# Projection tiles as 512-column matmuls on both weight parts, their halves added by VectorE, and the exponential's bias made by ScalarE

## The chip, the cores and the metric

The kernel runs on one core of a Trainium2 chip. The metric is the device time of one execution in microseconds; the number given for a kernel is the median of its runs. The profile is one execution taken apart by the hardware profiler. Its engines are PE (TensorE, matmuls; PEld is its weight load), DVE (VectorE), ACT (ScalarE), POOL (GpSimd) and SP (SyncE, which issues the DMAs).

## What is computed

One encoder layer on two groups of 1024 rows ("prompt", then "sample") that share their weights. Cut to what matters here:

```python
h = rms_norm(x, norm_g) * (1.0 + scale) + shift
proj = jnp.einsum('bsd,de->bse', h, w_in)              # 1024 -> 5376 columns
qa, ka, va, za, qb, kb, vb, zb, ga, gb = jnp.split(proj, ...)
qa, ka, qb, kb = rms_norm per head of 64, gain, rotary positions
oa = gqa_attention(qa, ka, va) * silu(za)              # 8 q heads, 2 kv heads
ob = rms_norm(diff_attention(qb, kb, vb, lam)) * silu(zb)   # 4 heads, two maps each
merged = sigmoid(ga) * (oa @ w_proj_a) + sigmoid(gb) * (ob @ w_proj_b)
y = x + gate * (merged @ w_out)
```

The softmax of a row of scores s is exp(rs * s - rs * max(s)), with rs the query row's inverse root mean square, which the kernel keeps apart and applies here.

## The kernel before

**Three products for one.** Every large product is made of 32-bit values that are split in a high part (a copy rounded to the matmul's type) and a low part (the rest): x * w becomes xh*wh + xh*wl + xl*wh, three matmuls added up in one PSUM bank. `split_w` (L190) splits a weight tile: ScalarE makes the high part (L195) and GpSimd or VectorE the low part (L197). A weight tile is laid out as [128, 8 chunks, 2 parts, 256 columns], so both parts of a chunk are 512 columns side by side.

**Projections by rows** (`proj_tt`, L565) are the place of the change. A tile is 128 rows of h by 256 columns of `w_in`. h (transposed, in `u` tiles) is the stationary side, so the result has rows on partitions. Over eight chunks of 128 channels run the three matmuls of L574, 128x256 each: 24 to a tile. The bank comes from `fbank`, a pool of three that projections, gates, transposes and others share. There are 72 such tiles to a group: 8 for k and v of branch A (`kva_gen`), 16 for its q (`qa_gen`), 32 for q and k of branch B (`qkb_gen`), 16 for its v (`vb_gen`).

**What reads a tile.** For v of branch B, one ScalarE copy (L749) takes it out of the bank. For q and k, `rms` (L586) does: ScalarE copies (L591) and squares (L592), VectorE sums the squares (L595) and adds epsilon (L596), GpSimd raises to the power -1/2 (L597), and `rope` rotates. In the heads of a group (`alone`) the rotation is VectorE's, elsewhere GpSimd's. `kva_gen` takes v out of the same bank by another ScalarE copy (L689). The rows then go back to TensorE to be transposed (`pairs_T`, L637), two tiles later (LAG).

**Softmax** (`softmax_unit`, L790). Four matmuls (L798, L799) fill one of two score banks `s` with 1024 scores for 128 rows. VectorE finds the negative maximum (L800) and scales it by rs (L801); ScalarE makes the exponential with it as bias (L802), which frees the bank. VectorE transposes the result in blocks of 32 (L843), DMAs carry it, and TensorE multiplies with the values (L866 and L883). There are 256 such units.

**The order of the work.** `weave` merges streams (attention steps, projections, gates by `z_gen` at L764) in shares that tables at the head of the file set, and the recorded program is then put in order engine by engine by a scheduler that follows priorities and its own idea of when operands are ready. Each engine runs its own list strictly in order. An edit to one function can therefore move instructions everywhere.

The functions that the change touches, and those that call them:

## Time and profile before

| | |
|---|---|
| median of 3 runs | 1882.31 us (1879.48 to 1884.93) |
| span of the profiled execution | 1880.0 us |
| TensorE busy | 98% of the span, 10398 matmuls |
| VectorE busy | 65% |
| ScalarE busy | 41% |
| GpSimd busy | 32% |
| mean granted clock of TensorE | 0.995 |

The span is the time from the first to the last instruction of the profiled execution; the runs were timed apart from it. A group row of the profile has the line, the engine, the operation, the tiles (out<-in), the shape and the count, then the busy time in us, the mean of one in ns, and the idle time of the engine ahead of these instructions with what ended most of it. Matmuls overlap each other in the array, so their busy time is longer than the time from one start to the next.

### The profile page before, as it was taken

The page shows a single profiled execution, that of the slowest core. Times are in us where ns is not written, and L with a number is a line of the kernel's source. Part 1 is how long each engine was busy: PE and PEld are TensorE (multiplying, and loading weights), DVE is VectorE, ACT ScalarE, POOL GpSimd, SP SyncE. Part 2 cuts the span into 40 slices and gives each one's busy share as a digit, 9 for nine tenths or more (in the row PEclk, how much of TensorE's full clock was granted, in tenths as well). Part 3 has the DMA queues.
Part 4 walks back from the last instruction along what each step waited for, and adds up shares of the span by engine and source line. Part 5 has one row for each costly group of instructions (what it writes and reads, how often), then busy time and mean ns, then how long its engine had stood idle before and what let it go on. Part 6 is the DMA issues. An engine that isn't in the chain of part 4 may idle for free.

```text
span 1880.0 us, 29891 instructions
## 1 busy us (share of the span) xinstructions
PE 1836.5 (98%) x10398; PEld 1550.6 (82%) x10398; DVE 1222.3 (65%) x2016; ACT 780.1 (41%) x1544; POOL 607.1 (32%) x888
## 2 busy tenths in 40 slices
PE   6999999999999999999999999999999999999999
PEld 3798877888899977888889888888888898888887
DVE  5777766454777777347466687666357766663795
ACT  4544434344554444313223445344345545442241
POOL 1243311433454451221233333014354635222100
PEclk8999999999999999999999999999999999999999
DMA  9135776555444567754631567666524343675442
GB/s 324 57 94 160 208 198 178 146 168 163 111 127 113 162 188 219 244 152 140 206 131 52 156 177 204 189 186 188 158 68 141 106 129 103 176 247 173 128 127 92
DMA packets 283895, 295.46 MB, mean 157 GB/s; under 512 B 41952, under 2 KB 236640, under 8 KB 283744
## 3 DMA queue, kind: packets, MB, share of 16 engines
q1 hardware_dynamic: 283744, 293.54, 53.1%
q8 instruction: 83, 1.36, 0.3%
q14 instruction: 68, 0.56, 0.1%
HBM read 133.98 MB, written 42.01 MB: 94 GB/s over the span
## 4 chain that ended last, share of the span: by engine, by line
PE 68%; DMA 4%; issue 3%; DVE 3%; SPq 3%; POOL 2%; ACT 1%; ACTq 0%; DVEq 0%; POOLq 0%
PE f L764 15%; PE f L574 15%; PE f L1038 7%; PE a L883 5%; PE s L798 4%; PE s L799 4%; PE a L866 4%; PE s L1038 3%; PE f L1073 3%; PE s L1073 2%; PE f L1145 2%; SPq L852 1%; DMA q<-p 1%; DMA st<-in_w_in_dram 1%; PE s L1145 1%
## 5 line engine op out<-in xcount | busy, mean ns | idle before, releaser
L764 PE MATMUL f<-u,w 128*128 128x512 f32 x2232 | 565.1, 395 | 0.8 <-POOL w L197 0.4
L574 PE MATMUL f<-w,u 128*128 128x256 f32 x3456 | 478.6, 287 | 0.9 <-POOL w L197 0.4
L764 PEld LDWEIGHTS f<-u,w 128*128 128x128 f32 x2232 | 409.8, 188 | 82.6 <-POOL w L197 1.1
L574 PEld LDWEIGHTS f<-w,u 128*128 128x128 f32 x3456 | 452.3, 193 | 22.3 <-issue 3.5
L800 DVE TENSOR_REDUCE m<-s 128x1 f32<-128x1024 f32 x256 | 309.6, 1218 | 98.8 <-PE s L799 97.4
L197 POOL TENSOR_TENSOR w<-st,w 128x512 fp32r<-128x512 f32 x160 | 213.2, 1350 | 357.9 <-ACT w L195 342.1
L843 DVE STREAM_TRANSPOSE p<-p 128x1024 f32<-128x1024 f32 x192 | 237.7, 1243 | 87.9 <-ACT p L802 73.5
L802 ACT ACTIVATE p<-s,m,u 128x1024 f32<-128x1024 f32 x128 | 153.9, 1204 | 160.0 <-issue 57.8
L802 ACT ACTIVATE p<-s,m,rsB 128x1024 f32<-128x1024 f32 x128 | 154.0, 1204 | 118.7 <-DVE m L801 97.1
L799 PE MATMUL s<-u,sw 128*128 128x512 f32 x512 | 201.1, 397 | 0.0
L195 ACT ACTIVATE w<-st 128x512 fp32r<-128x512 f32 x184 | 108.2, 626 | 112.4 <-DMA st<-in_w_in_dram 97.5
L1038 PE MATMUL f<-u,w 128*128 128x512 f32 x552 | 131.0, 392 | 0.0
L883 PE MATMUL a<-q,u 128*128 128x256 f32 x512 | 126.5, 380 | 4.0 <-DMA q<-p 3.7
L597 POOL TENSOR_TENSOR rsB<-ss,nhalf 128x4 f32<-128x4 f32 x64 | 68.1, 1064 | 184.7 <-DVE ss L596 160.6
L866 PE MATMUL a<-q,u 128*64 128x256 f32 x1024 | 117.7, 382 | 3.6 <-DMA q<-p 2.9
L1038 PEld LDWEIGHTS f<-u,w 128*128 128x128 f32 x552 | 103.0, 188 | 21.1
L798 PE MATMUL s<-u 128*128 128x512 f32 x256 | 107.9, 425 | 2.7 <-ACT p L802 2.7
L799 PEld LDWEIGHTS s<-u,sw 128*128 128x128 f32 x512 | 96.5, 189 | 16.4
L640 DVE TENSOR_TENSOR u<-f,u 64x256 fp32r<-64x256 f32 (+1 forms) x198 | 81.3, 411 | 42.9 <-ACT u L639 37.5
L883 PEld LDWEIGHTS a<-q,u 128*128 128x128 f32 x512 | 93.5, 190 | 18.8 <-issue 3.4
L772 ACT ACTIVATE ev<-f 128x512 f32<-128x512 f32 x93 | 55.3, 595 | 128.5 <-PE f L764 72.5
L866 PEld LDWEIGHTS a<-q,u 128*64 128x64 f32 x1024 | 73.8, 137 | 40.3 <-issue 7.2
(221 smaller groups left out, 2174.6 us busy)
## 6 DMA issues: line engine op xcount, KB each, us to landing
q<-p SPq DMA_DIRECT2D x768, 128.0 KB, 2.6
st<-in_w_in_dram SPq DMA_DIRECT2D x132, 256.0 KB, 3.3
zd<-ev SPq DMA_DIRECT2D x96, 256.0 KB, 2.7
sw<-u SPq DMA_DIRECT2D x256, 64.0 KB, 2.0
u<-in_w_ada_dram SPq DMA_DIRECT2D x8, 1024.0 KB, 11.7
oo<-zd SPq DMA_DIRECT2D x64, 128.0 KB, 2.4
od<-oo SPq DMA_DIRECT2D x64, 128.0 KB, 2.4
st<-in_w_in_dram SPq DMA_DIRECT2D x64, 128.0 KB, 2.7
```

The source lines that it names most:

```text
L195: hi = nc.scalar.activation(wh, st, AF.Copy)
L197: lo = e.tensor_tensor(out=wl, in0=st, in1=wh.bitcast(F32), op=ALU.subtract)
L574: ins = nc.tensor.matmul(ps, lt[c][:, sl], w[:, c, wi, :], start=(k == 0), stop=(k == 23))
L764: ins = nc.tensor.matmul(ps, w[:, c, wi, e * P : (e + 1) * P], rt[c], start=(k == 0), stop=(k == 23),)
L798: nc.tensor.matmul(s[:, sl], q, k[:, sl], start=True, stop=False)
L799: nc.tensor.matmul(s[:, sl], sw, k[:, sl], start=False, stop=True)
L800: nc.vector.tensor_reduce(out=m, in_=s, axis=AX.X, op=ALU.max, negate=True)
L802: nc.scalar.activation(pt.rearrange("p (j c a) -> p j c a", j=4, c=8), s.rearrange("p (c a j) -> p j c a", c=8, j=4), AF.Exp, bias=m, scal ...
L843: nc.vector.transpose(pt, pt)
L866: lambda k=k, m=m: nc.tensor.matmul(acc[(LO, HI)[m]], u["v"][:, k], pT[m][:, k], start=(k == 0), stop=(k == 7))
L883: nc.tensor.matmul(acc, u["v"][:, k], pT[:, k], start=(k == 0), stop=(k == 7))
L1038: nc.tensor.matmul(ps, w[:, c, wi, d * P : (d + 1) * P], o[:, oi, :], start=(k == 0), stop=(k == 11))
```

## The change

In `proj_tt` the high part of the rows now meets both weight parts in one matmul of 512 columns, and the low part meets the high weights in one of 256 columns that adds to the second half of the bank: 16 matmuls to a tile in place of 24. The bank then holds xh*wh in its first half and xh*wl + xl*wh in the second. A new function `summed` copies the first half out by ScalarE and lets VectorE add the second half to the copy, in place; `rms` and `vb_gen` use it in place of the single copy. In `kva_gen` v is copied from the summed row in SBUF instead of from the bank, inside `rms`. Epsilon is added by GpSimd instead of VectorE. In `softmax_unit` ScalarE scales the maximum by rs instead of VectorE.

```diff
     def proj_tt(ht, w, tt):
-        ps = fbank()[:, :256]
+        ps = fbank()
...
-            for lt, wi in ((hh, 0), (hh, 1), (hl, 0)):
-                ins = nc.tensor.matmul(ps, lt[c][:, sl], w[:, c, wi, :], start=(k == 0), stop=(k == 23))
+            both = w[:, c].rearrange("p s n -> p (s n)")
+            for lt, out, wt in ((hh, ps, both), (hl, ps[:, 256:], w[:, c, 0, :])):
+                ins = nc.tensor.matmul(out, lt[c][:, sl], wt, start=(k == 0), stop=(k == 15))
...
+    def summed(out, ps):
+
+        nc.scalar.activation(out, ps[:, :256], AF.Copy)
+        nc.vector.tensor_tensor(out=out, in0=out, in1=ps[:, 256:], op=ALU.add)
...
-    def rms(ps, nh, e, kept=None, first=0):
+    def rms(ps, nh, e, kept=None, first=0, vp=None):
...
-        nc.scalar.activation(raw, ps, AF.Copy)
+        summed(row[:, :256], ps)
+        if vp is not None:
+            nc.scalar.activation(vp, row[:, n:256].rearrange("p (h d) -> p h d", d=HD), AF.Copy)
...
-        nc.vector.tensor_scalar(out=ss, in0=ss, scalar1=EPS, scalar2=None, op0=ALU.add)
+        nc.gpsimd.tensor_scalar(out=ss, in0=ss, scalar1=EPS, scalar2=1.0, op0=ALU.add, op1=ALU.mult)
...
-            x3, s3 = rms(ps[:, :128], 2, e)
-            vp = ps[:, 128:256].rearrange("p (k d) -> p k d", k=2)
-            nc.scalar.activation(va[:, tt], vp, AF.Copy)
+            x3, s3 = rms(ps, 2, e, vp=va[:, tt])
...
-            nc.scalar.activation(v[:, tt].rearrange("p h e -> p (h e)"), ps, AF.Copy)
+            summed(v[:, tt].rearrange("p h e -> p (h e)"), ps)
...
-        nc.vector.tensor_tensor(out=m, in0=m, in1=rs, op=ALU.mult)
+        nc.scalar.activation(m, m, AF.Copy, scale=rs)
```

The lines below the edit move: L574 becomes L575, the copy and the sum of `summed` are L584 and L585, L800 to L802 become L806 to L808, L843 becomes L849.

What the order of the instructions becomes is shown at three places, all in the first group where v of branch B is projected beside attention. On TensorE before, one tile of v (`f_2923`), a gate (`f_2821`) and, further on, a score unit share the list; rows `x2` are two equal instructions:

```order
L574 MATMUL f_2923<-w_2610,u_511 128x256 x2
L574 MATMUL f_2923<-w_2610,u_512 128x256
L574 MATMUL f_2923<-w_2610,u_511 128x256
L764 MATMUL f_2821<-u_328,w_2804 128x512 x2
L764 MATMUL f_2821<-u_329,w_2804 128x512
L764 MATMUL f_2821<-u_328,w_2804 128x512
L574 MATMUL f_2923<-w_2610,u_511 128x256
L574 MATMUL f_2923<-w_2610,u_512 128x256
L574 MATMUL f_2923<-w_2610,u_511 128x256 x2
L574 MATMUL f_2923<-w_2610,u_512 128x256
```

On TensorE now, the same tile of v (it is called `f_2727` in the new program):

```order
L575 MATMUL f_2727<-w_2442,u_497 128x512
L575 MATMUL f_2727<-w_2442,u_498 128x256
L575 MATMUL f_2727<-w_2442,u_497 128x512
L575 MATMUL f_2727<-w_2442,u_498 128x256
L575 MATMUL f_2727<-w_2442,u_497 128x512
L575 MATMUL f_2727<-w_2442,u_498 128x256
L575 MATMUL f_2727<-w_2442,u_497 128x512
L575 MATMUL f_2727<-w_2442,u_498 128x256
L575 MATMUL f_2727<-w_2442,u_515 128x512
L804 MATMUL s_2413<-u_359,u_843 128x512
L805 MATMUL s_2413<-u_359,sw_2290 128x512
```

Two matmuls of 512 and 256 columns stand where three of 256 stood, and the gate no longer comes in between here; a score unit does.

On VectorE before, beside the same tile (`m` and `s` belong to score units, `p` to their exponentials, `oo` to a finished attention piece); the tile itself does not appear, since ScalarE took it out alone:

```order
L800 TENSOR_REDUCE m_2665<-s_2666 128x1
L801 TENSOR_TENSOR m_2665<-m_2665,u_360 128x1
L800 TENSOR_REDUCE m_2788<-s_2789 128x1
L843 STREAM_TRANSPOSE p_2664<-p_2664 128x1024
L801 TENSOR_TENSOR m_2788<-m_2788,u_360 128x1
L843 STREAM_TRANSPOSE p_2787<-p_2787 128x1024
L800 TENSOR_REDUCE m_2832<-s_2833 128x1
```

On VectorE now:

```order
L806 TENSOR_REDUCE m_2427<-s_2428 128x1
L806 TENSOR_REDUCE m_2487<-s_2488 128x1
L849 STREAM_TRANSPOSE p_2426<-p_2426 128x1024
L849 STREAM_TRANSPOSE p_2486<-p_2486 128x1024
L585 TENSOR_TENSOR u_2459<-u_2459,f_2727 128x256
L780 SCALAR_TENSOR_TENSOR ev_2803<-ev_2803,f_2734 128x512
L806 TENSOR_REDUCE m_2600<-s_2601 128x1
```

The scalings are gone from the list (the one of `m_2788` stood behind another unit's transpose), and the sum of the tile stands behind two reductions and two transposes.

On ScalarE before, the exponentials and the copy of the tile (L749):

```order
L802 ACTIVATE p_2664,suA_118<-s_2666,m_2665,u_360 128x1024
L802 ACTIVATE p_2787,suA_118<-s_2789,m_2788,u_360 128x1024
L749 ACTIVATE u_2627<-f_2923 128x256
L772 ACTIVATE ev_3006<-f_2933 128x512
L802 ACTIVATE p_2831,suA_118<-s_2833,m_2832,u_360 128x1024
```

On ScalarE now:

```order
L807 ACTIVATE m_2427<-m_2427,u_360 128x1
L808 ACTIVATE p_2426,suA_118<-s_2428,m_2427,u_360 128x1024
L807 ACTIVATE m_2487<-m_2487,u_360 128x1
L808 ACTIVATE p_2486,suA_118<-s_2488,m_2487,u_360 128x1024
L584 ACTIVATE u_2459<-f_2727 128x256
L778 ACTIVATE ev_2803<-f_2734 128x512
```

Each exponential has its scaling directly ahead of it, and the copy of the tile stands behind two such pairs.

## Prediction

> **What bounds the kernel now.** I read the page's head first (span, then busy time of each engine), then the granted clock, then the list of what TensorE waited for.
>
> ```profile
> span 1880.0 us, 29891 instructions
> PE 1836.5 (98%) x10398; PEld 1550.6 (82%) x10398; DVE 1222.3 (65%) x2016; ACT 780.1 (41%) x1544; POOL 607.1 (32%) x888
> ```
>
> The granted clock of the one core, and below it TensorE's waits, longest first (who waited, for whom, us in total, times, longest):
>
> ```profile
> core 0: 1880.0 us, clock 0.995
> ...
> PE f L330 <- ACT cT L384: 7.6, 1, 7.6
> PE s L798 <- ACT p L802: 4.2, 6, 1.2
> PE a L883 <- DMA q<-p: 3.7, 4, 1.5
> ...
> PE f L574 <- POOL w L197: 0.4, 1, 0.4
> ...
> PE f L574 <- ACT u L689: 0.3, 1, 0.3
> ```
>
> TensorE is busy for 98% of the span at a clock of 0.995, and its longest wait (7.6 us, at L330) lies before the first projection. Once the projections run, it waits 4.2 us in all for a score bank (L798, which ScalarE's exponential frees) and 0.3 us for a bank that an evacuation of a projection holds (L689). So the time is the sum of TensorE's paces. A nanosecond off the pace of a matmul moves the end; one off VectorE, ScalarE or GpSimd moves it only through a wait that this list does not have yet.
>
> The busy time of a matmul (287 ns at L574, below) counts its way through the array and overlaps the next one, so it is no price. The price is the distance from start to start, which the timeline of TensorE gives (start, length, line, count):
>
> ```profile
> 304.00 1.96 PE L574 MATMUL f<-w,u 128*128 128x256 f32 x15
> 305.79 2.23 PE L764 MATMUL f<-u,w 128*128 128x512 f32 x9
> 307.86 0.40 PE L574 MATMUL f<-w,u 128*128 128x256 f32 x2
> ...
> 1083.82 2.08 PE L574 MATMUL f<-w,u 128*128 128x256 f32 x16
> 1085.73 0.40 PE L798 MATMUL s<-u,u 128*128 128x512 f32 x1
> ...
> 1846.18 2.88 PE L1145 MATMUL s<-u,u 128*128 128x512 f32 x12
> 1848.90 2.88 PE L1145 MATMUL f<-u,q 128*128 128x512 f32 x12
> ...
> 127.26 0.28 PE L574 MATMUL f<-w,u 128*128 128x256 f32 x1
> 127.38 0.39 PE L798 MATMUL s<-u,u 128*128 128x512 f32 x1
> ```
>
> A run of 256-column matmuls paces at (305.79 - 304.00) / 15 = 119.3 ns and at (1085.73 - 1083.82) / 16 = 119.4 ns. A run of 512-column ones paces at (307.86 - 305.79) / 9 = 230 ns in the middle of the program and at (1848.90 - 1846.18) / 12 = 226.7 ns at its end. A single 256-column matmul with a 512-column one behind it takes 0.12 us too, so the paces add up when the two sizes alternate. Twice 119.4 is more than 230 and than 226.7: each instruction carries a part that does not depend on its columns, 2 x 119.4 - 230 = 8.8 ns by the one row and 2 x 119.4 - 226.7 = 12.1 ns by the other.
>
> **TensorE's part of the change.** The columns stay: three times 256 before, 512 + 256 after, for each 128 rows of the contraction. The instructions do not.
>
> ```profile
> L574 PE MATMUL f<-w,u 128*128 128x256 f32 x3456 | 478.6, 287 | 0.9 <-POOL w L197 0.4 <-ACT u L689 0.3 <-DVE ev L774 0.2
> L596 DVE TENSOR_SCALAR ss<-ss 128x4 f32<-128x4 f32 x96 | 21.3, 222 | 1.3
> L596 DVE TENSOR_SCALAR ss<-ss 128x2 f32<-128x2 f32 x16 | 3.1, 202 | 0.2
> L749 ACT ACTIVATE u<-f 128x256 f32<-128x256 f32 x32 | 12.1, 379 | 12.8 <-PE f L574 12.5
> L591 ACT ACTIVATE row<-f 128x256 f32<-128x256 f32 x96 | 36.7, 382 | 121.4 <-PE f L574 117.5 <-POOL row L600 2.9 <-POOL ssB L901 0.9
> ```
>
> 3456 matmuls are 144 tiles of 24 (96 + 16 that go through rms and 32 of the values). A tile now has 16, so 144 x 8 = 1152 matmuls and as many weight loads go. At 8.8 ns each that is 10.1 us, at 12.1 ns 13.9 us. A new tile is eight groups of 512 and 256 into one bank, a mix that no row shows over a length; I take 12.5 us, a little above the middle, because the steadier run gave the larger figure.
>
> The Trainium skill ("TensorE: Matmul & The Clock Gate", section "Back-to-back issue gap") states an isolated gap of N / 2.4 + 2.5 ns for a warm array, which by its own figures makes 109 and 216 ns; by it the change would save an estimated 1152 x 2.5 ns = 2.9 us. The rows above disagree with it (119.4 and 226.7 ns measured).
>
> **VectorE.** It adds 144 sums of 128x256 (one operand in PSUM, one in SBUF), and loses 256 scalings of the maximum (L801) and 112 additions of epsilon (L596).
>
> ```profile
> L640 DVE TENSOR_TENSOR u<-f,u 64x256 fp32r<-64x256 f32 x182 | 76.7, 422 | 39.1 <-ACT u L639 34.1
> L774 DVE SCALAR_TENSOR_TENSOR ev<-ev,f 128x512 f32<-128x512 f32 x29 | 19.6, 677 | 4.9 <-ACT ev L772 4.7
> L801 DVE TENSOR_TENSOR m<-m,u 128x1 f32<-128x1 f32 x128 | 28.2, 226 | 2.7
> L801 DVE TENSOR_TENSOR m<-m,rsB 128x1 f32<-128x1 f32 x128 | 26.6, 215 | 1.9
> L800 DVE TENSOR_REDUCE m<-s 128x1 f32<-128x1024 f32 x256 | 309.6, 1218 | 98.8 <-PE s L799 97.4
> L843 DVE STREAM_TRANSPOSE p<-p 128x1024 f32<-128x1024 f32 x192 | 237.7, 1243 | 87.9 <-ACT p L802 73.5 <-DMA q<-p 6.5 <-DMA sw<-u 1.7
> ```
>
> The sum has no row of its own. L640 has the same 256 columns and one operand in each memory (422 ns); L774 has twice the columns (677 ns) and bounds it from above. I take L640's: 144 x 0.422 = 60.8 us. Off go 28.2 + 26.6 + 21.3 + 3.1 = 79.2 us. VectorE ends at 1222.3 + 60.8 - 79.2 = 1204 us, less than now; even with 677 ns a piece (97.5 us) it would have 1241 us. Nothing of this is on TensorE's path in itself.
>
> **ScalarE and GpSimd.** ScalarE takes the 256 scalings, GpSimd the 112 additions.
>
> ```profile
> L487 ACT ACTIVATE lam<-lam x1: 203/203/203, 53.9 to 53.9; 128x2 f32<-128x2 f32 x1
> ...
> L802 ACT ACTIVATE p<-s,m,rsB 128x1024 f32<-128x1024 f32 x128 | 154.0, 1204 | 118.7 <-DVE m L801 97.1 <-issue 11.7 <-DMA q<-p 3.3
> L901 POOL TENSOR_TENSOR ssB<-ssB,suB 128x8 f32<-128x8 f32 x8 | 1.6, 204 | 25.5 <-DVE ssB L896 18.1 <-DVE m L801 7.3
> L900 POOL TENSOR_SCALAR suB<-suB 128x8 f32<-128x8 f32 x8 | 2.5, 309 | 0.7
> ```
>
> A two-element ScalarE instruction took 203 ns, so 256 of them are 52 us: 780.1 + 52 = 832 us, 44% of the span. A small GpSimd instruction took 204 to 309 ns; 112 of them are 23 to 35 us and GpSimd ends near 635 us. Both engines keep more than half of the span free, which hides this; without that cover it would cost up to 87 us.
>
> On the chain maximum - scaling - exponential, 0.20 us on ScalarE stand where 0.22 us on VectorE stood, so its length stays. Two things about queues change. Before, the scaling could stand in VectorE's queue behind a reduction or a transpose of another unit (1218 and 1243 ns), and the exponential waited for it: 97.1 us of ScalarE's idle time in the group of branch B is put down to it. That goes. In its place ScalarE's queue now stops at the scaling until the reduction is done, where it used to stop at the exponential: the same instructions stand behind it (evacuations of projections, halves of transposed q and k).
>
> In rms two more handoffs stand ahead of ScalarE's square: it waits for VectorE's sum, and behind it in ScalarE's queue stand exponentials; and VectorE's sum waits for ScalarE's copy, with reductions and transposes behind it. That lengthens the way of a tile to its transposes on TensorE by 0.42 us and what the sum stands behind. These come two tiles later (LAG), 2 x 2.87 = 5.7 us of TensorE's time by the pace above, so I cost it at nothing; without that cover it would be 0.42 us for each of 112 tiles, 47 us.
>
> The kva values copy (L689) now reads the summed row in SBUF, not the bank; its 16 pieces are late by the sum, and are needed only when the value matmuls start.
>
> **The new wait.** A bank of a projection tile was free after one copy of about 0.38 us. Now it is held by that copy and, behind it, by VectorE's sum of 0.42 us, which can stand behind a reduction or a transpose: between 0.42 us and 0.42 + 1.22 + 1.24 = 2.9 us longer. There are three such banks. One tile of 24 matmuls is 24 x 119.4 = 2.87 us of TensorE's time, and before its bank is due again two others are normally filled, so some 5 us of cover stand against a hold of 0.8 to 3.3 us. The cover is thinner in the two heads, where tile follows tile and VectorE also does the rotations:
>
> ```profile
> 60.00:150.00 90.00, 88.20 (x583) 80.22 (x583) 69.46 (x173) 45.90 (x117) 34.09 (x38) 0.99 0.28 80
> 1010.00:1100.00 90.00, 90.00 (x565) 78.04 (x564) 64.13 (x127) 39.78 (x86) 30.58 (x37) 1.00 0.45 125
> 1300.00:1500.00 200.00, 195.13 (x1178) 168.50 (x1176) 123.49 (x213) 95.78 (x197) 99.72 (x187) 1.00 0.44 124
> ```
>
> In the first head VectorE is busy 69.5 us of 90. Its 16 tiles add 16 x (0.42 - 0.22) = 3.2 us, 81%, still under TensorE's share. In the attention stages (123.5 of 200 us) VectorE gets lighter. From below the cost of the new hold is nothing; from above I take one wait of 1.2 us (a reduction) for about one tile in twenty, 7 x 1.2 = 8 us. I charge 1.5 us: the present list has 0.3 us of such waits, and the cover is normally several times the hold.
>
> **The sum.** 1880.0 - 12.5 + 1.5 = 1869.0 us of span. The median of the three runs, 1882.31, lies 2.3 us above this profile's span, so the forecast is 1871 us, 11 us or 0.6% faster. A measurement of this kernel can tell about 0.3% (5.6 us) from no change, so faster is below 1876.7 and slower above 1888.
>
> **Rivals.**
>
> *The waits eat the gain.* The longer hold of the bank costs its upper bound of 8 us or a little more: 1880.0 - 12.5 + 8 to 12 + 2.3 = 1878 to 1882 us, no change that can be told. For it: the first head's VectorE at over 80%. Against it: two other banks stand between. Chance 0.13.
>
> *The saving was never per instruction.* If the new mix paces with the columns alone (a 512-column matmul behind a 256-column one at 2 x 119.4 = 239 ns), nothing is removed: 1880.0 + 1.5 + 2.3 = 1884 us. Against it: 230 ns in the middle of the program, between two runs of L574. Chance 0.04. The gap formula of the Trainium skill's page "TensorE: Matmul & The Clock Gate" (section "Back-to-back issue gap") comes near this case, with its 2.9 us.
>
> *Slower: VectorE's queue stops the projections.* The sum waits in order behind a reduction whose scores TensorE makes only after the tile, and TensorE, coming back for the bank, waits for both. In the new order of VectorE 17 of the 144 sums stand behind such a reduction. If each of them holds TensorE for a reduction (1.22 us), that is 20.7 us: 1880.0 - 12.5 + 20.7 + 2.3 = 1890.5 us. The point from which it decides is 12.5 us / 144 = 0.09 us of new wait per tile. Against it: TensorE makes those scores before it comes back for the bank, so the reduction and the sum run beside it. Chance 0.08.
>
> *More than the matmuls.* The exponential no longer waits for a scaling behind another unit's transpose, so the score waits (4.2 us) and some of the value matmuls' waits for the flipped exponentials (3.7 us, L883) go as well, with the full 13.9 us: 1880.0 - 13.9 - 4.2 - 3.7 + 2.3 = 1860.5 us. For it: ScalarE's 97.1 us behind L801. Against it: those waits are few, since the filler matmuls cover the chain. Chance 0.09.
>
> **How the numbers follow.** The forecast with its bounds (saving 10.1 to 13.9 us, new waits 0 to 5 us) reaches from 1868 to 1877 us and has 0.66; 0.02 of it, with the small saving and the large wait, counts as no change. Faster: 0.64 + 0.09 and 0.02 of the first rival with a smaller wait = 0.75. Same: 0.02 + 0.11 + 0.04 = 0.17. Slower: 0.08. The range goes from 1863 us (half of the last rival's way below the forecast) to 1881 us (most of the first rival); it leaves out the slower case, the column pace and the rest of the fourth.
>
> **What would show it.** In the changed kernel's timeline a tile's 512 and 256 pairs should start 8 x (226.7 + 119.4) = 2.77 us apart over a whole tile, against 2.87; TensorE's waits for projection banks, named after the new sum, should stay under some 3 us; VectorE's busy time should be near 1204 us, ScalarE's near 832, GpSimd's near 635; the sum should take about 422 ns and the scaling about 203. The prediction is wrong if a pair paces at 358 ns, if TensorE's list gains a row of over 8 us that ends in VectorE's sum, or if the stages without projections, which have nothing to save, change in length as much as those with them.

## The result, and the profile after

The changed kernel took 1894.74 us (median of 4 runs, 1894.51 to 1897.45) beside 1881.02 for the kernel before in the same session: a ratio of 1.0077, 95% interval 1.0062 to 1.0091. It is slower by some 14 us where 11 us faster was forecast, and lies outside the range. All ratios compare undisturbed runs of both kernels on one chip, so one need not be the quotient of two medians.

The head of the page and the granted clock of the changed kernel:

```profile
span 1895.7 us, 27956 instructions
...
PE 1839.6 (97%) x9246; PEld 1490.7 (79%) x9246; DVE 1216.7 (64%) x1792; ACT 855.9 (45%) x1800; POOL 635.0 (33%) x1000
```

```profile
core 0: 1895.7 us, clock 0.993
```

1152 matmuls went, as the change says, and the span grew by 15.7 us. Where it grew can be read from when TensorE starts the same instruction in the two kernels. First the kernel before (its first score, the start of the merge of the first group, the last tile of the out stage behind it, the merge of the second group), then the changed one:

```profile
127.38 0.39 PE L798 MATMUL s<-u,u 128*128 128x512 f32 x1
...
793.74 3.02 PE L1038 MATMUL f<-u,w 128*128 128x512 f32 x12
...
965.29 5.60 PE L1073 MATMUL f<-u,w 128*128 128x512 f32 x24
...
1705.25 0.58 PE L1038 MATMUL f<-u,w 128*128 128x512 f32 x1
```

```profile
133.68 0.39 PE L804 MATMUL s<-u,u 128*128 128x512 f32 x1
...
805.20 3.02 PE L1044 MATMUL f<-u,w 128*128 128x512 f32 x12
...
976.75 5.60 PE L1079 MATMUL f<-u,w 128*128 128x512 f32 x24
...
1720.89 0.58 PE L1044 MATMUL f<-u,w 128*128 128x512 f32 x1
```

The changed kernel is 6.3 us late at the first score, 11.5 at the first merge, still 11.5 at the end of the out stage (976.75 - 965.29), 15.6 at the second merge. The stages without projections cost nothing; the loss lies in the first head (6.3 us), the first group's attention (5.2) and the second group (4.2). TensorE has the same work behind it at each of these points in both kernels, to within two matmuls at the first score. TensorE's waits name what ended it (who waited, for whom, us in total, times, longest):

```profile
PE f L645 <- DVE row L634: 10.3, 4, 4.7
...
PE s L804 <- ACT p L808: 7.0, 6, 2.7
PE f L770 <- DVE row L585: 3.7, 3, 2.3
PE f L575 <- POOL w L197: 3.4, 2, 2.8
...
PE f L575 <- DVE row L585: 0.3, 1, 0.3
```

The projections hardly wait for a bank (the last row). The transposes (L645) wait for the rotated row, a later step than the sum; the gates (L770) for a bank that the sum holds.

The largest single wait shows the way. VectorE in the changed kernel, then GpSimd, then TensorE, 83 to 95 us:

```profile
87.09 0.42 DVE L585 TENSOR_TENSOR row<-row,f 128x256 f32<-128x256 f32 x1 [0.16 <-ACT row L584]
87.43 0.28 DVE L628 TENSOR_TENSOR rc<-row,tab 128x128 f32<-128x128 f32 x1
87.63 1.43 DVE L633 TENSOR_TENSOR row<-row,tab 128x64 f32<-128x64 f32 x2
88.98 1.76 DVE L197 TENSOR_TENSOR w<-st,w 128x512 fp32r<-128x512 f32 x1
90.67 0.28 DVE L634 TENSOR_TENSOR row<-rc,row 128x128 f32<-128x128 f32 x1
```

```profile
87.66 2.54 POOL L197 TENSOR_TENSOR w<-st,w 128x512 fp32r<-128x512 f32 x2 [1.38 <-ACT w L195]
```

```profile
86.42 0.27 PE L645 MATMUL s<-ident,row 128*128 128x128 f32 x1
91.09 0.45 PE L645 MATMUL f<-ident,row 128*128 128x128 f32 x1 [4.40 <-DVE row L634]
91.19 3.83 PE L770 MATMUL f<-u,w 128*128 128x512 f32 x9
```

And the kernel before in the same place, VectorE and then TensorE:

```profile
85.14 0.35 DVE L625 TENSOR_TENSOR row<-row,tab 128x64 f32<-128x64 f32 x2
85.53 0.29 DVE L626 TENSOR_TENSOR row<-rc,row 128x128 f32<-128x128 f32 x1
```

```profile
85.96 0.30 PE L637 MATMUL f<-ident,row 128*128 128x128 f32 x1
86.02 5.28 PE L764 MATMUL f<-u,w 128*128 128x512 f32 x22
```

Before, the rope's steps took 0.35 + 0.29 us and the transposes followed at once, with 22 gate matmuls behind them. After, a later tile's sum (87.09) stands ahead of these steps; by then GpSimd makes low weight parts (87.66, two instructions in 2.54 us), and the same two steps take 1.43 us. A low part of the weights (L197) stands ahead of the last step, and TensorE waits 4.40 us with its gates behind the transpose. The Trainium skill ("SBUF — State Buffer", section "SBUF: two separate sides") says that VectorE and GpSimd share a pair of ports that one instruction locks for its whole length, a VectorE one with two SBUF operands included when the GpSimd one reads SBUF. The 1.43 against 0.35 us beside GpSimd's L197 agrees with it; no run here was made to take that lock apart, though e10 below bears on it.

Such a wait is paid for again in the clock. The windows behind it, changed kernel (stretch, length, busy time of the five engines, granted clock):

```profile
86.00:91.00 5.00, 0.69 (x5) 0.39 (x3) 4.69 (x10) 2.49 (x7) 2.81 (x3) 1.00 0.00 0
91.00:95.00 4.00, 3.91 (x11) 3.18 (x12) 2.81 (x10) 1.45 (x4) 0.89 (x2) 0.57 0.62 197
95.00:100.00 5.00, 5.00 (x30) 4.28 (x29) 2.04 (x6) 0.70 (x3) 3.08 (x5) 1.00 0.19 57
...
60.00:150.00 90.00, 83.01 (x420) 69.83 (x419) 69.27 (x163) 45.55 (x113) 36.87 (x52) 0.96 0.23 68
```

For the 4 us after the wait the granted clock is 0.57, which takes another (1 - 0.57) x 4 = 1.7 us, and it is 0.96 over the first head where before had 0.99. The Trainium skill ("TensorE: Matmul & The Clock Gate", section "What's actually happening") lets the clock fall to half after an idle window of about 3.4 us; this trace agrees (4.40 us of waiting, then 0.57 over 4 us).

The groups that the forecast sized (mean ns after the comma):

```profile
L575 PE MATMUL f<-w,u 128*128 128x512 f32 x1152 | 423.9, 404 | 4.3 <-POOL w L197 3.4 <-DVE u L648 0.6 <-DVE row L585 0.3
...
L807 ACT ACTIVATE m<-m,u 128x1 f32<-128x1 f32 x128 | 37.2, 291 | 145.4 <-DVE m L806 141.4 <-POOL row L634 3.8
...
L585 DVE TENSOR_TENSOR row<-row,f 128x256 f32<-128x256 f32 x112 | 46.0, 412 | 65.2 <-ACT row L584 64.0
```

and a run of TensorE, with the next start below it:

```profile
1521.19 6.29 PE L575 MATMUL f<-w,u 128*128 128x256 f32 x35
1527.32 0.50 PE L900 MATMUL f<-ones_c,at 128*128 128x1 f32 x4
```

35 matmuls are 17 pairs and one of 256 columns: (1527.32 - 1521.19 - 0.12) / 17 = 354 ns a pair. Over all pairs in the trace the commonest distance from pair to pair is 350 ns, where three matmuls of 256 take 3 x 119.4 = 358 and 346 was forecast. The pace of 230 ns gives 230 + 119.4 = 349 ns.

### The profile page after: what moved, and what is told of

Same layout as the page of the kernel before. It is cut to its first block, busy times and chain, and to the rows that moved or that the text cites. A ratio compares the mean times of both kernels' runs of the same rounds, so it can differ in the third digit from the quotient of the medians.

```text
span 1895.7 us, 27956 instructions
## 1 busy us (share of the span) xinstructions
PE 1839.6 (97%) x9246; PEld 1490.7 (79%) x9246; DVE 1216.7 (64%) x1792; ACT 855.9 (45%) x1800; POOL 635.0 (33%) x1000
## 4 chain that ended last, share of the span: by engine, by line
PE 77%; DMA 7%; DVE 7%; ACT 3%; SPq 2%; POOL 2%; issue 2%; POOLq 0%; ACTq 0%; DVEq 0%
PE f L770 21%; PE f L575 18%; PE f L1044 7%; PE a L872 6%; PE s L804 5%; PE s L805 5%; PE a L889 4%; PE s L1044 3%; DMA q<-p 2%; PE f L1151 2%; DMA st<-in_w_in_dram 2%; PE s L1151 1%; SPq L858 1%; PE s L1079 1%; PE f L1079 1%
## 5 line engine op out<-in xcount | busy, mean ns | idle before, releaser
L770 PE MATMUL f<-u,w 128*128 128x512 f32 x2232 | 569.3, 398 | 6.6 <-DVE row L585 3.7
L770 PEld LDWEIGHTS f<-u,w 128*128 128x128 f32 x2232 | 414.5, 190 | 94.8 <-DVE row L585 4.4
L575 PE MATMUL f<-w,u 128*128 128x512 f32 (+1 forms) x2304 | 457.0, 344 | 4.3 <-POOL w L197 3.4
L575 PEld LDWEIGHTS f<-w,u 128*128 128x128 f32 x2304 | 368.8, 190 | 63.2 <-POOL w L197 4.1
L806 DVE TENSOR_REDUCE m<-s 128x1 f32<-128x1024 f32 x256 | 309.0, 1218 | 86.9 <-PE s L805 84.6
L197 POOL TENSOR_TENSOR w<-st,w 128x512 fp32r<-128x512 f32 x160 | 213.6, 1354 | 450.3 <-ACT w L195 309.9
L849 DVE STREAM_TRANSPOSE p<-p 128x1024 f32<-128x1024 f32 x192 | 238.6, 1243 | 68.0 <-ACT p L808 62.6
L808 ACT ACTIVATE p<-s,m,rsB 128x1024 f32<-128x1024 f32 x128 | 154.1, 1204 | 4.8 <-DMA q<-p 1.6
L808 ACT ACTIVATE p<-s,m,u 128x1024 f32<-128x1024 f32 x128 | 154.3, 1205 | 3.8 <-ACT m L807 0.2
L604 POOL TENSOR_SCALAR ss<-ss 128x4 f32<-128x4 f32 (+1 forms) x112 | 27.8, 249 | 268.7 <-DVE ss L603 256.4
L807 ACT ACTIVATE m<-m,u 128x1 f32<-128x1 f32 x128 | 37.2, 291 | 145.4 <-DVE m L806 141.4
```

The source lines that it names most:

```text
L197: lo = e.tensor_tensor(out=wl, in0=st, in1=wh.bitcast(F32), op=ALU.subtract)
L575: ins = nc.tensor.matmul(out, lt[c][:, sl], wt, start=(k == 0), stop=(k == 15))
L770: ins = nc.tensor.matmul(ps, w[:, c, wi, e * P : (e + 1) * P], rt[c], start=(k == 0), stop=(k == 23),)
L806: nc.vector.tensor_reduce(out=m, in_=s, axis=AX.X, op=ALU.max, negate=True)
L808: nc.scalar.activation(pt.rearrange("p (j c a) -> p j c a", j=4, c=8), s.rearrange("p (c a j) -> p j c a", c=8, j=4), AF.Exp, bias=m, scal ...
L849: nc.vector.transpose(pt, pt)
```

## The experiments

The theories, with the letters of the expectations. **A**: the sum costs, by the longer way of a row to its transposes (A-chain), by VectorE's queue (A-queue) or by the longer hold of the bank (A-hold). **B**: the scaling on ScalarE stops its queue. **C**: the scheduler remakes the order of all engines around any edit, and the order by itself is worth time. **D**: GpSimd's addition of epsilon costs.

**One part at a time, in the scheduler's own order.** `e1_matmul_only` is before with the merged matmuls and the sum; `e2_bias_only` before with the scaling on ScalarE; `e3_eps_only` before with epsilon on GpSimd; `e4_no_bias` the changed kernel with the scaling back on VectorE. The edits of the two middle ones:

```diff
-        nc.vector.tensor_tensor(out=m, in0=m, in1=rs, op=ALU.mult)
+        nc.scalar.activation(m, m, AF.Copy, scale=rs)
...
-        nc.vector.tensor_scalar(out=ss, in0=ss, scalar1=EPS, scalar2=None, op0=ALU.add)
+        nc.gpsimd.tensor_scalar(out=ss, in0=ss, scalar1=EPS, scalar2=1.0, op0=ALU.add, op1=ALU.mult)
```

> The kernel before with the matmul part alone: 16 matmuls to a tile and VectorE's sum of the halves; epsilon and the scaling of the maximum stay on VectorE. Theory A (the sum lengthens the way of a tile's rows, and TensorE, which keeps its list in order, waits for transposes and banks): about as slow as the changed kernel, 1889 to 1897 us. Theory B (the scaling on ScalarE stops ScalarE's queue; the matmul part is the gain that was forecast): 1868 to 1875 us. Theory C (any edit reshuffles the scheduler's order, and the waits that come of it have little to do with what was edited): anywhere from 1872 to 1895 us, and the four kernels of this call don't add up to the changed one.

> The kernel before with the scaling of the maximum on ScalarE, nothing else. Theory A: 1878 to 1884 us, no change. Theory B: 1890 to 1900 us, since nothing pays for the stopped queue. Theory C: off by several us to either side.

> The kernel before with epsilon added by GpSimd, nothing else: 112 small instructions move from VectorE to GpSimd. Theories A and B: 1878 to 1884 us, no change. Theory C: off by several us to either side though hardly anything is changed.

> The changed kernel with the scaling of the maximum back on VectorE (matmul part and epsilon on GpSimd stay). Theory A: 1889 to 1897 us, as the changed kernel. Theory B: 1868 to 1876 us. Theory C: anywhere from 1872 to 1895 us.

Measured: e1 1914.72 us (ratio 1.0176, 1.0163 to 1.0189), e2 1890.14 (1.0045, 1.0029 to 1.0060), e3 1909.03 (1.0146, 1.0132 to 1.0159), e4 1911.71 (1.0154, 1.0141 to 1.0167). Each part alone is slower, and three kernels with part of the change are slower than the whole: 33 + 8 + 27 us against 14. Parts of a cost that belongs to the instructions would add up. The waits of e3, where 112 instructions of 0.2 us changed engine:

```profile
PE a L866 <- DMA q<-p: 6.3, 6, 1.7
PE a L883 <- DMA q<-p: 5.2, 5, 1.8
```

The waits that grew (value matmuls on the flipped exponentials, 2.9 and 3.7 us before) have nothing to do with epsilon: the sign of theory C.

**The order held.** To take C out, a function chains each engine's instructions in a listed order, that of before; what the edit adds is put where it becomes ready.

```diff
+def held(nc, tc):
...
+    for engine, text in HELD.items():
...
+            if prev is not None:
...
+                tc.add_manual_dep(ins, prev.name, dep)
+            prev = ins
...
         tile_encoder_layer_kernel(tc, aps)
+        held(nc, tc)
```

`e5_eps_held` and `e7_bias_held` are e3 and e2 in the order of before, `e6_change_held` the whole change in it (each sum stands in VectorE's list where the copy ended). `e8_one_share` is before with the first number of the weave's table of shares (ATT_W) at 1.02 and not 1.0, with no instruction altered.

> Epsilon on GpSimd, as in the run of that part alone, which took 1909 us, but every engine keeps the order of instructions of the kernel before (TensorE, ScalarE and the DMA queue row for row; the 112 additions leave VectorE's list and stand directly ahead of their powers in GpSimd's). Theory C (the remade order costs the time, not the instruction that moved): 1878 to 1886 us. Theory D (GpSimd's addition itself delays the rows: 112 x 0.25 us and what waits for them): 1900 to 1912 us, order or not.

> The whole change with the order of the kernel before: on TensorE every third matmul of a group goes and nothing else moves; the sums are put into VectorE's list where the copy used to end, the scalings directly ahead of their exponentials. Theory C: TensorE keeps its saving of some 6 to 10 us less a few short waits, 1868 to 1880 us, faster than both kernels. Theory A (the sum itself lengthens the rows' way and TensorE waits): 1888 to 1897 us, as the changed kernel.

> The scaling of the maximum on ScalarE, as in the run of that part alone (1890 us), with the order of the kernel before: TensorE and the DMA queue row for row, each scaling directly ahead of its exponential. Theory C: 1876 to 1884 us. Theory B (the scaling stops ScalarE's queue): 1888 us or more.

> The kernel before with one number of its tables changed by 2% (the first share of attention in the first group, 1.0 to 1.02): no instruction is added, removed or altered, only the order moves, on TensorE in 1160 of 9486 places. Theory C: off by 5 us or more, most likely slower, since the tables were set by the order that they make. If order matters little: 1878 to 1885 us.

Measured: e5 1883.56 (1.0001, 0.9988 to 1.0014), e7 1882.48 (0.9998, 0.9981 to 1.0015), e6 1892.28 (1.0049, 1.0031 to 1.0066), e8 1888.83 (1.0022, 1.0005 to 1.0039). With the order held, epsilon and the scaling are free to within 3 us: the 27 and 8 us of e3 and e2 came with the remade order, and B and D fall. e8 shows the order at work with no edit at all, by a smaller amount. But the change as a whole stays 9 us slower in the order of before, so C is not all: the matmuls and the sum together carry a cost of their own.

**The sum against the matmuls.** `e9_no_sum_held` is e6 without the sum (it leaves out the two products with low parts); `e11_24_matmuls_held` is e6 with three matmuls of 256 columns into the two halves; `e10_copy_all_held` frees the bank by ScalarE alone.

```diff
 e9
-        nc.vector.tensor_tensor(out=out, in0=out, in1=ps[:, 256:], op=ALU.add)
 e11
-            for lt, out, wt in ((hh, ps, both), (hl, ps[:, 256:], w[:, c, 0, :])):
+            for lt, out, wt in ((hh, ps[:, :256], both[:, :256]), (hh, ps[:, 256:], both[:, 256:]), (hl, ps[:, 256:], w[:, c, 0, :])):
 e10
-        nc.scalar.activation(out, ps[:, :256], AF.Copy)
-        nc.vector.tensor_tensor(out=out, in0=out, in1=ps[:, 256:], op=ALU.add)
+        nc.scalar.activation(row, ps, AF.Copy)
+        nc.vector.tensor_tensor(out=out, in0=row[:, :256], in1=row[:, 256:], op=ALU.add)
```

> The whole change in the order of before, without VectorE's sum: ScalarE copies the first half alone, so the results lack the two products with the low parts. TensorE's matmuls are those of the change (1152 of 512 columns and 1152 of 256). If the one-matmul form saves TensorE what the modes of its steps in the changed kernel's trace give (117 + 233 = 350 ns against 358 ns for the three, 1152 times: 9.4 us) and only the sum gave it back, this kernel is at about 1873 us, ratio 0.994 to 0.997. If TensorE saves nothing, it is within 0.1% of before (1880 to 1884). If the bank is what costs (the accumulator takes a bank's whole row in both halves), it stays slower, 1886 or more. The profile of the projections must show no wait on a row from VectorE that before did not have.

> The change in the order of before, with the three matmuls of 256 columns that before has: the product of the two high parts into the first half of the bank, the two others into the second, then the copy and VectorE's sum as in the change. TensorE saves nothing here, so it shows what the sum costs by itself: before plus what the sum costs. If the sum costs the 10 us by which the held change is slower plus the 6 to 9 us that TensorE saves, 1898 to 1902 us, ratio 1.008 to 1.010. If TensorE saves nothing in the held change, the same time as that, 1890 to 1894 (1.004 to 1.006). If the sum costs nothing, 1882 to 1884.

> The whole change in the order of before, but ScalarE copies all 512 columns out of the bank and VectorE adds the two halves in SBUF: the bank is given back by ScalarE alone, after a longer copy, and the sum still stands in the row's chain. Theory A-hold (the sum keeps the bank too long, and the next tile's first matmul waits for VectorE): waits of L575 on the sum go to zero and the time falls from the 1892 of the held change to 1878 to 1885, ratio 0.998 to 1.001. Theory A-chain (the bank does not matter; the transposes and the gates come late because the row is ready some 0.9 us or more later, behind VectorE's queue): 1890 to 1896, ratio 1.004 to 1.008, with the waits of the transposes on the row still there.

Measured: e9 0.9977 (0.9965 to 0.9989), e11 1.0067 (1.0054 to 1.0081), e10 1.0079 (1.0065 to 1.0092). Two ways to the same numbers: without the sum the merged matmuls gain 0.0023 x 1882 = 4.3 us, and against e11 they gain (1.0067 - 1.0049) x 1882 = 3.4 us; the sum costs 12.6 us over before (e11) and (1.0049 + 0.0023 - 1) x 1882 = 13.5 us over e9. A-hold, which expected 1878 to 1885 us, fails in e10 (1899.24 us): the projections' waits for the sum's bank, 3.2 us in e6, are gone, 1.1 us of waits for the copy stand in their place, and the kernel is no faster, slower if anything. But e10 does not price the hold by itself. Its copy is longer, and its sum has both operands in SBUF. The sum of q and k rows in e6, then in e10 (ns, least/median/most):

```profile
L585 DVE TENSOR_TENSOR row<-row,f x112: 379/420/424, 49.3 to 1593.8; 128x256 f32<-128x256 f32 x112
```

```profile
L585 DVE TENSOR_TENSOR row<-row x112: 380/424/1483, 49.4 to 1602.7; 128x256 f32<-128x256 f32 x112
```

With one operand in the bank no sum took over 0.42 us; with both in SBUF some take up to 1.48. In e9 one wait grew:

```profile
PE f L575 <- POOL w L197: 4.7, 6, 1.2
```

Before it was 0.4 us, once: TensorE comes earlier for weight parts that GpSimd still makes, and gives part of its gain back there. Other waits became shorter.

**Another order of the changed kernel.** `e12_after_share` makes e8's edit in the changed kernel.

> The changed kernel as it is, with one number of the weave's table of shares at 1.02 and not 1.0: no instruction is another, only the order moves. Theory C (what order the scheduler happens on is worth some us either way): 1885 to 1905 us, a ratio 0.003 or more away from the changed kernel's 1.0077. If the order is worth nothing and the sum alone makes the change slower, it stays within 0.002 of 1.0077, at 1893 to 1899 us.

Measured: 1895.22 us (1.0062, 1.0049 to 1.0076). That is the changed kernel's time again; here the order was worth nothing, where C had expected 0.003 or more.

**By which way the sum costs.** `e13_sum_aside_held`: VectorE adds a constant to the second half of the bank in place, and no row waits for it. `e17_add_elsewhere`: a reduction of 256 columns of a table in SBUF, at the same places, tied to no bank. `e15_copy_all_no_sum`: e9 with a copy of 512 columns for each row. All three leave out the low parts.

```diff
 e13
-        nc.vector.tensor_tensor(out=out, in0=out, in1=ps[:, 256:], op=ALU.add)
+        low = ps[:, 256:].rearrange("p (a n) -> p a n", a=2)
+        nc.vector.tensor_tensor(out=low, in0=ident.unsqueeze(1).to_broadcast([P, 2, P]), in1=low, op=ALU.add)
 e17
-        nc.vector.tensor_tensor(out=out, in0=out, in1=ps[:, 256:], op=ALU.add)
...
+        nc.vector.tensor_reduce(out=idle[:, at : at + 2], in_=twice, axis=AX.X, op=ALU.add)
 e15, from e9
-        nc.scalar.activation(out, ps[:, :256], AF.Copy)
+        nc.scalar.activation(row, ps[:, : row.shape[-1]], AF.Copy)
```

> The change in the order of before, but VectorE's add works on the bank's second half in place (a constant is added to it), and the rows go on from the first half alone, so that the low parts are left out: VectorE does the same 144 adds of 256 columns out of the same bank, the bank is kept as long, but no row waits for them. Before's time is taken as 1882, the run without any sum as 1879, the held change as 1892. Theory A-chain (the longer way from the last matmul to the transposes is what costs): 1877 to 1882, ratio 0.997 to 1.000. Theory A-queue or A-hold (other work on VectorE stands behind the add, or the next tile waits for the bank): 1888 to 1893, ratio 1.003 to 1.006. In between, both share it.

> The held change with VectorE's sum replaced by a reduction of 256 columns of a constant table in SBUF (about 0.42 us each, 144 times, at the same places in VectorE's list); it waits for nothing, keeps no bank, and no one reads it, and the low parts are left out. If VectorE's time is what costs the 8 us of the sum set aside: as that run, 1885 to 1888 (ratio 1.001 to 1.003). If the tie to the bank is what costs (the wait at its place, the bank kept): as the run without a sum, 1878 to 1881 (0.997 to 0.999).

> The run without the sum (1879.67, ratio 0.9977), with ScalarE copying 512 columns and not 256 for each of the 112 rows (about 0.2 us more in the row's way, the bank kept as much longer, VectorE untouched; the low parts are left out as in that run). If a way longer by some tenths of a us is what costs, whichever engine makes it longer: 1882 to 1887, ratio 1.000 to 1.003. If it must be VectorE's time that costs: unchanged, 1878 to 1881 (0.997 to 0.999).

Measured: e13 1.0018 (1.0006 to 1.0031), e17 1.0014 (1.0003 to 1.0024), e15 0.9989 (0.9979 to 1.0000). e13 falls between what A-chain and what A-queue or A-hold expected; e17 and e15 fall where it is VectorE's time that costs. e17's group row gives what was added, 0.40 us a piece:

```profile
L590 DVE TENSOR_REDUCE idle<-ident 128x2 f32<-128x256 f32 x144 | 57.4, 402 | 0.4
```

Laid one on the other, as shares of 1882 us: merged matmuls -4.3 us (e9); VectorE's time (e17 over e9) +7.0; the tie to the bank (e13 over e17) +0.8; the row's longer way (e6 over e13) +5.8; the scheduler's own order (changed kernel over e6) +5.3. They add up to the whole loss, 14.6 us, because each starts where the one before it ends; that is no check of them. A difference of two such ratios is uncertain by about 0.002 (3 to 4 us). So VectorE's time is shown to cost (the intervals of e9 and e17 lie apart). The row's way is not: the intervals of e13 and e6 touch, and e15's longer copy, which lengthens that way, is not told apart from e9. The bank's tie is no different from nothing, and the intervals of e6 and the changed kernel overlap.

TensorE's idle time is a second reading of the same steps. From 40 us on, where the projections begin, to the end of the span (stretch, length, busy time of the five engines, granted clock), for before, e9, e17, e13, e6 and the changed kernel:

```profile
40.00:1880.00 1840.00, 1814.07 (x10289) 1539.47 (x10288) 1201.51 (x1979) 766.15 (x1520) 598.43 (x876) 1.00 0.53 153
...
40.00:1878.90 1838.90, 1811.84 (x9138) 1481.58 (x9137) 1144.41 (x1612) 840.39 (x1776) 622.92 (x988) 0.99 0.52 153
...
40.00:1880.80 1840.80, 1806.32 (x9140) 1477.36 (x9139) 1186.70 (x1757) 840.07 (x1776) 623.01 (x988) 1.00 0.54 153
...
40.00:1884.20 1844.20, 1810.57 (x9138) 1477.38 (x9137) 1193.70 (x1756) 839.85 (x1776) 622.45 (x988) 0.99 0.52 152
...
40.00:1888.20 1848.20, 1812.41 (x9138) 1477.63 (x9137) 1196.21 (x1756) 842.70 (x1776) 622.18 (x988) 0.99 0.52 152
...
40.00:1895.70 1855.70, 1814.43 (x9138) 1478.86 (x9137) 1196.01 (x1757) 841.93 (x1776) 626.42 (x988) 0.99 0.51 151
```

The length less TensorE's busy time (the second and third figure) is 25.9 us before, 27.1 in e9, 34.5 in e17, 33.6 in e13, 35.8 in e6 and 41.3 in the changed kernel. VectorE's time adds 7.4 us here too; the spans of these two profiles lie only 1.9 us apart (1878.9 and 1880.8) because e9's ran at the lower clock (0.99 against 1.00). The row's way adds 2.2 us and the scheduler's order 5.5. These are single profiles: e5 and e7, which took before's time, have 27.3 and 28.7 us, so 2.2 us is no difference. From e9 to e17 the waits that grow most are those of the value matmuls for the flipped exponentials (5.6 to 9.3 us in all); those of the transposes for the rows grow from 7.6 to 8.7.

**Three remedies.** `e14_sum_after_rope` is e6 with 7 sums put behind an earlier row's rope steps. `e16_lag3` is the changed kernel with the transposes three tiles behind, in the scheduler's own order. `e18_sum_gpsimd` is e10 with the sum on GpSimd.

```diff
 e16
-LAG = 2
+LAG = 3
 e18, from e10
-        nc.vector.tensor_tensor(out=out, in0=row[:, :256], in1=row[:, 256:], op=ALU.add)
+        nc.gpsimd.tensor_tensor(out=out, in0=row[:, :256], in1=row[:, 256:], op=ALU.add)
```

> The whole change in the order of before, with 7 of the 144 sums moved in VectorE's list behind the rope steps of an earlier row that stood next to them, among them the one at 1005 us, where the rope waited 0.45 us for a sum and then fell behind GpSimd's making of weight parts, and the transposes waited 3.9 us. If the sum costs by standing in VectorE's queue ahead of steps that TensorE waits for: 3 to 5 us below the held change's 1892, at 1887 to 1889 (1.002 to 1.004). If the queue is not what costs there, no change: 1890 to 1894 (1.004 to 1.006).

> The changed kernel in its own order, with the transposes of a row issued three tiles behind its projection and not two: 2.8 us more time for the sum and what follows it. The scheduler remakes the order, which by itself moved other variants by 0 to 30 us. Theory A-chain: the waits of the transposes on the row (10.3 us in the changed kernel) go, and the kernel comes to 1876 to 1888, ratio 0.997 to 1.003. If the row's way is not what costs: 1890 to 1905 (1.004 to 1.012), with other waits in their place.

> The whole change in the order of before, with ScalarE copying all 512 columns and GpSimd, not VectorE, adding the halves in SBUF. The longer copy cost 2 us without a sum; the row's way is longer still by GpSimd's add (an estimate from its rope steps of the same shape: 0.6 to 0.7 us against VectorE's 0.42), and GpSimd's weight parts stand behind it. If VectorE's time was the dearest part: 1884 to 1889 (1.001 to 1.004), below the 1899 of the same copy with VectorE's sum. If the row's way is: 1895 to 1905 (1.007 to 1.012).

Measured: e14 1891.23 (1.0045, 1.0029 to 1.0060), e16 1906.02 (1.0117, 1.0098 to 1.0137), e18 1907.46 (1.0131, 1.0115 to 1.0147). e14 comes out where "no change" was expected: the wait it aimed at shrank and another came right behind it, so the queue at these seven places is not shown to cost anything. The held change, then e14, around 1008 us:

```profile
1008.53 0.30 PE L645 MATMUL f<-ident,row 128*128 128x128 f32 x1 [3.91 <-DVE row L634]
```

```profile
1008.24 0.30 PE L645 MATMUL f<-ident,row 128*128 128x128 f32 x1 [0.80 <-DVE row L634]
1009.84 2.55 PE L575 MATMUL f<-w,u 128*128 128x512 f32 x12 [1.30 <-POOL w L197]
```

e16 misses the 1876 to 1888 us of A-chain: the transposes wait 3.9 us where the changed kernel had 10.3, but the gates now wait 5.2 us for VectorE's half of the transposed rows, and the kernel is slower.

```profile
PE f L770 <- DVE u L648: 5.2, 4, 1.7
...
PE f L645 <- DVE row L634: 3.9, 2, 3.4
```

How much of e16's 22 us is the lag and how much the remade order isn't settled: before with a lag of three was not run. e18 takes the sums off VectorE, puts a step of 0.79 us into the row's way and is the slowest of the held kernels. That fits a cost of the row's way, but GpSimd, which also makes weight parts, is busy 109 us longer (739.6 against 630.8 in e6), and the two are not told apart:

```profile
L585 POOL TENSOR_TENSOR row<-row 128x256 f32<-128x256 f32 x112 | 88.4, 790 | 182.6 <-ACT row L584 182.6
```

No version with the whole computation beat the kernel before.

## Why the prediction was wrong

**The step that failed** is the price of VectorE's sums. An added step off TensorE was to cost "only through a wait that this list does not have yet". So 60.8 us of sums were set off against 79.2 us of VectorE steps that go ("Nothing of this is on TensorE's path in itself"), the longer way of the rows was costed "at nothing" behind 5.7 us of cover, and the one charge was 1.5 us for the bank. Measured, the sum costs 12.6 us (e11) or 13.5 (e6 over e9), and TensorE idles 15.3 us more in the changed kernel than before (41.27 against 25.93), 0.11 us a tile, above the 0.09 from which the prediction said that such waits decide. Some 7 us of the sum's cost are VectorE's time (e17 over e9); how the rest divides between the row's way and the bank stays open. VectorE's total says nothing of it: e5 and e7 took 55 us of VectorE's work away and gained nothing, and 144 steps of 0.40 us that nobody waited for cost 7 us. So it seems to matter where on VectorE's list a step stands; no run tests which places.

The list did have waits for VectorE and for the rows. These rows of the kernel before stood between the ones quoted and were passed over:

```profile
PE f L637 <- POOL row L626: 3.4, 2, 3.2
...
PE f L637 <- DVE row L626: 2.5, 2, 1.4
PE s L637 <- DVE row L626: 1.6, 1, 1.6
```

7.5 us of waiting for the row at five places say that the cover of two tiles was already spent there, so that more work ahead of the row can be paid in full. The changed kernel has 10.3 us of such waits at four places. They are one part of the loss: e9, without any sum, has 7.6 us of them and e6 9.5.

**TensorE's saving**, 12.5 us, came to 4.3 (e9), with an interval of 2 to 7 us. A pair takes 350 to 354 ns and not 346, so by the commonest distance the paces give 1152 x 8 = 9 us. The prediction had two paces of 512 columns, 230 and 226.7 ns, both from runs of 512 columns alone, and chose nearer the larger saving; the pair came out by the 230 ns, the smaller one. Of the other 5 us, some 1 us is TensorE's longer idle time in e9 (27.06 against 25.93 us); where the rest goes is open.

**The order.** The sum had no term for it. That the scheduler remakes all lists was shown with the change and priced at nothing. In parts of the change it was worth 8 to 27 us with no other cost in them (e2 against e7, e3 against e5). In the whole change it may be about 5 us (1.0077 against 1.0049, 5.5 us of idle time); the intervals overlap, so this is not shown.

**The new wait on the bank** was charged at 1.5 us with an upper bound of 8. The changed kernel waits 0.3 us at L575 and 3.7 at the gates, which share the banks, 4.0 us in all; e6 waits 3.2 us at L575. That is more than the charge and inside the bound. What the tie costs in time, e13 against e17, is 0.8 us, no different from nothing. **The rival that was slower** came near in time (1890.5 us), but by 20.7 us of waits for a bank behind VectorE's queue, of which 4.0 came; that its time fits is luck. **The fourth rival** let the score waits and the value matmuls' waits go. The second fell from 6.6 to 3.9 us, the first rose from 4.2 to 7.0.

**The loads.** GpSimd at 635.0 us was right. The sum took 412 ns (422 forecast). ScalarE came to 855.9 us and not 832, since the scaling takes 291 ns and not the 203 of a two-element row. VectorE came to 1216.7 and not 1204: e7 and e5, without the sum, have it at 1182.3 and 1207.0, so the parts that go took 40.0 and 15.3 us off, 55 and not 79 us, and e6 has 51.8 us more than e9 (1216.8 and 1165.0), so the sums added 52 and not 61 us (the busy time of short instructions that overlap is counted once). That these moves cost nothing was right (e5, e7), but only in the old order.

**The test** that the prediction gave itself did not find the error. None of its three signs came: a pair does not pace at 358 ns, no wait of TensorE that ends in the sum itself reached 8 us, and the loss lies in the stages with projections. Waits for banks that the sum holds came to 4.0 us with those of the gates, where some 3 was the limit. The time was lost in waits that end in other steps of VectorE and of what it feeds, and the largest row, 10.3 us, ends in the rotation.

## What to carry to other kernels

Before an added step is costed at nothing, look in the bounding engine's waits for any row that ends in the chain it joins: here waits of up to 3.2 us at five places showed that the cover was used up there, with VectorE busy for 65% of the span. An engine's busy time summed over the span does not price a step either: here 55 us less gained nothing, and 52 us more, in the sums, came with a cost of 13. In a program that a scheduler orders, price the remade order too, and hold the old one before an edit's own cost is read: here single edits with no cost of their own moved the time by 8 to 27 us. A pace for a mix of sizes is best taken from a run of that mix; without one, the row that saves less is the safer choice.

## What the runs showed of the hardware

- A matmul of 512 columns and one of 256 on the same bank, in turn, take 350 to 354 ns a pair, 4 to 8 ns more than the separate paces (226.7 + 119.4 = 346). Against 3 x 119.4 = 358 ns, a merge of two 256-column matmuls saved 4 to 8 ns and not 11.
- A wait of TensorE of 4.40 us was followed by 4 us at a granted clock of 0.57, another 1.7 us.
- Two VectorE steps that took 0.35 us together before took 1.43 us while GpSimd worked on 512-column weight parts. This is the longest wait of the first head. The change's sum, with one operand in the bank, took at most 0.42 us in e6; the same sum with both operands in SBUF took up to 1.48 us in e10.
- A scaling of one element a partition took ScalarE 291 ns, where the two-element instruction of before took 203.
